# A fused macaron layer on one core: large tiles moved to multiples of 512 bytes, lone blocks rounded ahead of sums, rotary tables computed beside the down products

## The chip, the cores and the metric

One core of a Trainium2 chip runs the whole layer as one launch. The metric is device time in microseconds (us). The time before is 1897.17 us, the median of three runs (1897.16 to 1900.1).

## The reference, cut to what matters

Everything is float32; 256 tokens, model width 2048, feed-forward width 5632. The layer is a feed-forward block, a mixing block (retention with eight heads beside a sparse attention with eight heads), and a second feed-forward block, each with a residual sum.

```
def swiglu(h, w_gate, w_up, w_down):
    return (jax.nn.silu(h @ w_gate) * (h @ w_up)) @ w_down

x = x + 0.5 * swiglu(rmsnorm(x, ffn1_norm), w_gate1, w_up1, w_down1)
proj = rmsnorm(x, mix_norm) @ w_in                  # 2048 -> 6992 columns
rq, rk, rv, rg, aq, ak, av, iq, ik, iw = split(proj)
...
x = x + concatenate([ro, ao]) @ w_out
x = x + 0.5 * swiglu(rmsnorm(x, ffn2_norm), w_gate2, w_up2, w_down2)
return rmsnorm(x, final_norm)
```

`rq`, `rk`, `aq`, `ak`, `iq` and `ik` are rotated by position (`rope`), with cosines and sines of position times frequency, once for heads of 128 and once for heads of 64.

## The kernel before, in words

**Products.** Every float32 weight is read once from HBM by SP's queue, 1 MB at a time, into one of three `raw` buffers. A load is cut into pieces, and for each piece ScalarE (ACT) writes the rounded part `hi` (line 280) and VectorE (DVE) the rest `lo = raw - hi` (line 286), both in the one-pass format fp32r, into five buffers each. The activations are split in the same way. A product is then three TensorE (PE) matmuls, hi·hi, hi·lo and lo·hi, added up in PSUM: `run_mms` (line 232) with the weights streaming (512 columns each) and the activations stationary. In the input projections of the mixing block it is the other way round (`mm_cols`, lines 145 to 148: `hi` and `lo` stationary, `xg` streaming), save for two of them (`mm_rows`, lines 163 to 165).

**S and C pairs.** The products of the feed-forward blocks and of `w_out` take the depth in pairs of 256 rows. A C pair is done plainly, with 24 matmuls. An S pair follows Strassen's scheme with seven block products, 21 matmuls: DVE first forms four differences of weight blocks (line 272), and the activation side needs four sums besides the blocks that stand alone. `blocks_of` (lines 303 to 322) makes both sides of it for one pair: DVE forms the sums in `f`, ACT rounds the sums, ACT rounds the lone blocks, DVE subtracts twice. `left_pair` calls it for the products of a chunk after PE has transposed them (line 560).

**Order.** A feed-forward block has eleven chunks of 512 gate and 512 up columns, in two parts of six and five, and each part ends with its two down products. A chunk after the first has 3 S and 5 C pairs, 183 matmuls of 512 columns; the first is plain, 192. The product of a chunk is transposed and split in the middle of the next one (`sums_of`, `turning`); of its two pairs the first is an S pair in chunks one to four of each part, as the strings `DOWN` say. So 16 chunks in the two blocks have the split of an S pair in them, here called S-turn chunks. Everything is issued in an order fixed by hand: `after(step, ...)` hangs work on a piece, pieces are split four ahead of PE, and each engine runs its instructions in order.

**Addresses.** The built program places the tiles of a pool behind each other in the order of their first use. `gains` and `cst` stand ahead of `x0`, so that in pool `one` the large tiles (`x`, `xg`, `ext`, `ident`) begin 416 bytes past a multiple of 512; four small `r_tok` tiles at its end put `raw`, `hi`, `lo` and `mid` 32 bytes past one. Every operand of a large matmul is a whole number of 512-byte steps from its tile's start, so it has the same remainder (those of lines 163 to 165 with 272 columns excepted). `xg` and `ext` hold the activations for the gate, up and mixing products; `mid` holds those for the down products and `w_out`, and for three of the eight pairs of the first chunk.

**Tables.** `tables` (lines 641 to 681) computes angles, their reduction to one turn, and sines as a chain of DVE operations on 1024 elements, during the second part's first chunks of the first block; at that part's down product ACT's Sin writes them to `ext["rot"]`, in the space that the split `x` held until then.

Of the kernel before, what the change touches and what calls it, by code (L numbers as in the profile page):

```python
# [11 lines left out]
F32 = mybir.dt.float32  # L12
F32R = mybir.dt.float32r
I32 = mybir.dt.int32
AF = mybir.ActivationFunctionType
OP = mybir.AluOpType
# [3 lines left out]
P = 128  # L20
T = 256
# [20 lines left out]
C_TWO_PI = 2.0 * math.pi  # L42
C1 = 6.28125
C2 = round((C_TWO_PI - C1) * 2**17) / 2**17
C3 = C_TWO_PI - C1 - C2
MAGIC = 1.5 * 2**23
PI_DOWN = 3.1415925
# [3 lines left out]
def layer(ctx: ExitStack, tc: tile.TileContext, a: dict, out: bass.AP):  # L51
    nc = tc.nc
    V, S, G, TE = nc.vector, nc.scalar, nc.gpsimd, nc.tensor

    one = ctx.enter_context(tc.tile_pool(name="one", bufs=1))
    wts = ctx.enter_context(tc.tile_pool(name="wts", bufs=4))
    mid = ctx.enter_context(tc.tile_pool(name="mid", bufs=16))
    tmp = ctx.enter_context(tc.tile_pool(name="tmp", bufs=2))
    psum = ctx.enter_context(tc.tile_pool(name="psum", bufs=1, space=PSUM))
    ctx.enter_context(tc.manual_schedule())  # L60

# [2 lines left out]
    def new(pool, shape, dt=F32, tag=None, bufs=None):  # L64
        count[0] += 1
        kw = {} if bufs is None else {"bufs": bufs}
        return pool.tile(shape, dt, name=f"{tag}_{count[0]}", tag=tag, **kw)

    def half_k(tag, bufs=2):
        return new(tmp, [P, 2, T], F32, tag, bufs)  # L70

    def big(dt=F32, shape=(P, 4, T)):
        return new(mid, list(shape), dt, "mid")


    gains = new(one, [P, 3 * KT + NH], F32, "gains")
    cst = new(one, [P, 4 + NH], F32, "cst")
    x = [new(one, [P, D], F32, f"x{t}") for t in range(2)]
    xg = {}

# [6 lines left out]
    now, marks = [0], {}  # L87
# [16 lines left out]
    def after(step, fn):  # L104
        ends.setdefault(step, []).append(fn)
# [197 lines left out]
    def blocks_of(v, sums, alone):  # L303

        v = v.rearrange("p j (t n) -> p j t n", t=2)
        f = new(tmp, [P, 4, P], F32, "sq")
        V.tensor_tensor(f[:, 0], v[:, 0, 1], v[:, 1, 1], op=OP.add)
        V.tensor_tensor(f[:, 2], v[:, 0, 1], v[:, 0, 0], op=OP.subtract)
        V.tensor_tensor(f[:, 1], f[:, 0], v[:, 0, 0], op=OP.subtract)
        V.tensor_tensor(f[:, 3], v[:, 1, 0], f[:, 1], op=OP.subtract)  # L310
        vt = v.rearrange("p k t n -> p t k n")
        S.activation(sums[:, :, 0], f, AF.Copy)
        if alone.shape[1] == 4:
            a4 = alone.rearrange("p (t k) h n -> p t k h n", t=2)
            S.activation(a4[:, :, :, 0], vt, AF.Copy)  # L315
            V.tensor_tensor(a4[:, :, :, 1], vt, a4[:, :, :, 0].bitcast(F32), op=OP.subtract)  # L316
        else:
            for o, w in ((slice(0, 2), vt[:, 0]), (slice(2, 3), vt[:, 1, 1:2])):
                S.activation(alone[:, o, 0], w, AF.Copy)
                V.tensor_tensor(alone[:, o, 1], w, alone[:, o, 0].bitcast(F32), op=OP.subtract)  # L320
        V.tensor_tensor(sums[:, :, 1], f, sums[:, :, 0].bitcast(F32), op=OP.subtract)
        return sums, alone

    def left_pair(kind, v, in_psum=True):

        if kind == "S":
            if in_psum:
                f = half_k("b")
                S.activation(f, v, AF.Copy)
                v = f  # L330
            return blocks_of(v, big(F32R, (P, 4, 2, P)), big(F32R, (P, 4, 2, P)))
        t = big(F32R, (P, 2, 512))
        S.activation(t[:, :, :T], v, AF.Copy)
        V.tensor_tensor(t[:, :, T:], v, t[:, :, :T].bitcast(F32), op=OP.subtract)
        return t
# [18 lines left out]
    def s_of_x(c, norm, xT):  # L354
        v = half_k("b")
        for j in range(2):
            S.activation(v[:, j], xT[:, j], AF.Copy, scale=gain(norm, c, j))
        xs[c] = blocks_of(v, new(one, [P, 4, 2, P], F32R, f"xg{c}"), x_ext(c))
# [12 lines left out]
    ext = {}  # L371
# [7 lines left out]
    def mix_ext():  # L379
        t = new(one, [P, EXT], F32, "ext")  # L380
        at = 0
        for name, n in (("rot", 4 * T), ("avw", 2 * W_AV), ("ikT", T), ("score0", P), ("score1", T)):
            ext[name] = t[:, at:at + n]
            at += n
        ext["rot"] = ext["rot"].rearrange("p (k t) -> p k t", k=4)
        ext["avw"] = ext["avw"].rearrange("p (t n) -> p t n", t=2)
        ext["x"] = None
# [27 lines left out]
    def rsqrt(o, v, n):  # L415

        q = new(tmp, [P, 2 * NH], F32, "rs_q", 1)[:, :n]
        S.activation(q, v, AF.Sqrt)
        V.reciprocal(o, q)
        V.scalar_tensor_tensor(q, o, -0.5, o, op0=OP.mult, op1=OP.mult)  # L420
        V.tensor_tensor(q, q, v, op=OP.mult)
        V.scalar_tensor_tensor(o, q, 1.5, o, op0=OP.add, op1=OP.mult)

    def act_table(fn):

        t = new(tmp, [P, 1], F32, "table", 1)
        S.activation(t, ones[:, 0:1], fn)

    r_tok, r_of = {}, {}

    def row_of(tok):

# [9 lines left out]
    def rstd_tok(norm, ts=slice(0, 2)):  # L442
        v = new(tmp, [P, 2], F32, "sum_v", 1)[:, ts]
        s, k = squares[norm]
        V.tensor_reduce(v, s[:, ts, :k[ts.start]], axis=AX.X, op=OP.add)
        V.tensor_scalar(v, v, 1.0 / D, EPS, op0=OP.mult, op1=OP.add)
        if norm not in r_tok:
            r_tok[norm] = new(one, [P, 2], F32, f"r_tok{norm}")
        rsqrt(r_tok[norm][:, ts], v, ts.stop - ts.start)

    def rstd(norm):
        rstd_tok(norm)
        row = yield from row_of(r_tok[norm])
        r_of[norm] = new(tmp, [P, T], F32, "r", 1)
        S.activation(r_of[norm], row, AF.Copy)
# [182 lines left out]
    inv, sgn, kdec = cst[:, 0:2], cst[:, 2:4], cst[:, 4:4 + NH]  # L638


    def tables(at_sin):
        ang, n = big(), big()
        pi, pf = n[:, 0].bitcast(I32), n[:, 1]
        G.dma_start(pi, bass.AP(tensor=a["pos"].tensor, offset=a["pos"].offset, ap=[[0, P], [1, T]]))
        yield 3
        V.tensor_copy(pf, pi)
        for k in range(2):
            for j in range(2):
                V.tensor_scalar(ang[:, 2 * k + j], pf, inv[:, k:k + 1], None, op0=OP.mult)
        yield 3  # L650
        V.tensor_scalar(n, ang, 1.0 / C_TWO_PI, None, op0=OP.mult)
        yield 3
        for k in range(2):
            V.tensor_scalar(n[:, 2 * k], n[:, 2 * k], 0.25, None, op0=OP.add)
        yield 3
        V.tensor_scalar(n, n, MAGIC, None, op0=OP.add)
        yield 3
        V.tensor_scalar(n, n, MAGIC, None, op0=OP.subtract)
        for c in (C1, C2, C3):
            yield 3  # L660
            V.scalar_tensor_tensor(ang, n, -c, ang, op0=OP.mult, op1=OP.add)
        for k in range(2):
            V.tensor_scalar(ang[:, 2 * k], ang[:, 2 * k], math.pi / 2, None, op0=OP.add)
        yield 3

        V.tensor_scalar(n, ang, 1.0 / C_TWO_PI, MAGIC, op0=OP.mult, op1=OP.add)
        yield 3
        V.tensor_scalar(n, n, MAGIC, None, op0=OP.subtract)
        for c in (C1, C2, C3):
            yield 3  # L670
            V.scalar_tensor_tensor(ang, n, -c, ang, op0=OP.mult, op1=OP.add)
        yield 3
        V.tensor_scalar(ang, ang, PI_DOWN, -PI_DOWN, op0=OP.min, op1=OP.max)
        yield 3
        yield at_sin - now[0]
        mix_ext()
        rot = ext["rot"]
        S.activation(rot, ang, AF.Sin)
        yield 2
        for k in range(2):  # L680
            V.tensor_scalar(rot[:, 2 * k + 1], rot[:, 2 * k + 1], sgn[:, k:k + 1], None, op0=OP.mult)


    def first_squares():
        for t in range(2):
            nc.sync.dma_start(x[t], a["x"][t])
        yield 4
        for t in range(2):
            for c in range(2):
                square_x(0, t, 1024 * c, 1024)  # L690
                yield 1
        rstd_tok(0)

    after(FIRST_SQ, first_squares)
    end = ffn(1, 0, 1, False)
    after(marks[1, 1] + 2, lambda: tables(marks[1, 1, "down"] + 2))


    m0 = len(pieces)
# [355 lines left out]
    n = len(pieces)  # L1055
# [100 lines left out]
```

## Time and profile before

| | |
|---|---|
| median of three runs | 1897.17 us |
| the profiled execution: its time, its span | 1896.84 us, 1895.1 us |
| PE matmul, DVE, ACT busy | 98%, 87%, 57% of the span |
| DMA | 359 MB, 190 GB/s, engines busy half of the time |
| granted TensorE clock | 0.998 |

The page gives busy shares of the whole span. The timeline lists instructions of one engine with their start, so the distance from one matmul's start to the next is what a matmul takes in a row of them (its own duration overlaps the next). An idle time in brackets is the engine's wait before the instruction, with what ended it.

### The profile page before, as it was taken

Reading aid. Unit: us, or ns where it says so; the run is one execution under the profiler, and the core shown is the slowest. Engines: PE = TensorE matmul, PEld = TensorE weight load, DVE = VectorE, ACT = ScalarE, POOL = GpSimd, SP = SyncE. Lnnn points to the kernel's source line nnn. Section 1 sums busy time; section 2 is a strip of 40 time slices with the busy share of each in tenths; the row PEclk is TensorE's granted clock in tenths of the full one; section 3 lists DMA queues with packets and bytes.
Section 4 is the critical chain, followed back from the end, with each engine's and each line's share of the span. In section 5 each row is a group of like instructions: output and inputs, shape, how many; then the busy total and the mean of one; then the engine's idle time right before and its main releaser. Section 6 shows DMA issues by size and latency. Waiting matters only on the chain.

```text
span 1895.1 us, 22782 instructions
## 1 busy us (share of the span) xinstructions
PE 1862.9 (98%) x8643; PEld 1525.0 (80%) x8643; DVE 1646.2 (87%) x2109; ACT 1072.9 (57%) x1351; POOL 5.3 (0%) x14
## 2 busy tenths in 40 slices
PE   9999999999999999999999999999999999999997
PEld 7877788887777787988888888877778888777786
DVE  7899998889999997789865786799999889999998
ACT  7655555545555565656654566555555455555564
POOL 0000000000000000000000000000000000000000
PEclk9999999999999999999999999999999999999999
DMA  8544556545455454545434364545554555445554
GB/s 312 199 178 178 199 197 221 194 173 195 182 201 197 165 212 156 188 164 207 178 137 174 134 222 156 200 178 196 201 200 180 200 200 200 178 181 202 194 180 176
DMA packets 51885, 359.33 MB, mean 190 GB/s; under 512 B 5920, under 2 KB 5920, under 8 KB 9280
## 3 DMA queue, kind: packets, MB, share of 16 engines
q1 hardware_dynamic: 50976, 355.62, 50.7%
q8 instruction: 67, 1.10, 0.2%
q10 hardware_dynamic: 432, 1.08, 0.2%
q0 software_dynamic: 368, 1.19, 0.2%
q14 instruction: 42, 0.34, 0.0%
HBM read 355.76 MB, written 2.10 MB: 189 GB/s over the span
## 4 chain that ended last, share of the span: by engine, by line
PE 75%; DVE 19%; ACT 3%; issue 2%; DMA 0%; SPq 0%; DVEq 0%; ACTq 0%
PE M L232 58%; DVE lo L286 8%; PE M L146 8%; PE M L148 4%; DVE raw L272 3%; DVE e L471 2%; ACT hi L280 1%; DVE s L471 1%; PE M L164 1%; PE M L165 1%; PE M L163 1%; DVE x L468 1%; PE M L560 1%; DVE mid L316 1%; ACT mid L315 1%
## 5 line engine op out<-in xcount | busy, mean ns | idle before, releaser
L280 ACT ACTIVATE hi<-raw 128x1024 fp32r<-128x1024 f32 (+2 forms) x859 | 848.3, 1008 | 567.0 <-DVE raw L272 366.4
L286 DVE TENSOR_TENSOR lo<-raw,hi 128x1024 fp32r<-128x1024 f32 (+2 forms) x859 | 978.3, 1159 | 121.9 <-ACT hi L280 107.9
L232 PE MATMUL M<-hi,xg 128*128 128x512 f32 x2240 | 739.2, 396 | 1.4 <-DVE e L471 1.0
L232 PE MATMUL M<-hi,mid 128*128 128x512 f32 x1690 | 528.2, 391 | 4.1 <-DVE e L986 1.7
L232 PEld LDWEIGHTS M<-hi,xg 128*128 128x128 f32 x2240 | 421.7, 188 | 102.8 <-DVE e L471 5.3
L232 PE MATMUL M<-lo,xg 128*128 128x512 f32 x1120 | 443.6, 396 | 5.8 <-DVE lo L286 5.7
L232 PEld LDWEIGHTS M<-hi,mid 128*128 128x128 f32 x1690 | 317.2, 188 | 73.8 <-DVE e L986 2.1
L232 PE MATMUL M<-lo,mid 128*128 128x512 f32 x845 | 329.5, 390 | 1.5 <-DVE lo L286 1.4
L272 DVE TENSOR_TENSOR raw<-raw 128x512 f32<-128x512 f32 x380 | 262.9, 692 | 12.7
L232 PEld LDWEIGHTS M<-lo,xg 128*128 128x128 f32 x1120 | 211.0, 188 | 60.3 <-DVE lo L286 13.0
L146 PE MATMUL M<-xg,hi 128*128 128x512 f32 x688 | 245.1, 398 | 1.2 <-DVE xg L300 1.1
L232 PEld LDWEIGHTS M<-lo,mid 128*128 128x128 f32 x845 | 158.7, 188 | 35.9 <-DVE lo L286 3.5
L148 PE MATMUL M<-xg,lo 128*128 128x256 f32 x645 | 182.1, 282 | 0.0
L146 PEld LDWEIGHTS M<-xg,hi 128*128 128x128 f32 x688 | 128.3, 188 | 30.4 <-DVE xg L300 1.8
L232 PE MATMUL M<-hi,ext 128*128 128x512 f32 x360 | 143.5, 399 | 1.9
L148 PEld LDWEIGHTS M<-xg,lo 128*128 128x128 f32 x645 | 121.3, 188 | 0.8
L232 PEld LDWEIGHTS M<-hi,ext 128*128 128x128 f32 x360 | 67.8, 188 | 23.2 <-DVE s L471 8.0
L232 PE MATMUL M<-lo,ext 128*128 128x512 f32 x180 | 71.1, 395 | 0.0
L471 DVE TENSOR_TENSOR s<-s,M 128x512 f32<-128x512 f32 x98 | 65.5, 683 | 2.2 <-PE M L232 1.2
L550 ACT ACTIVATE s<-s,r_tok 128x512 f32<-128x512 f32 x40 | 27.1, 720 | 54.6 <-DVE s L471 54.6
L471 DVE TENSOR_TENSOR e<-s,M 128x512 f32<-128x512 f32 x58 | 39.6, 684 | 1.0
L232 PEld LDWEIGHTS M<-lo,ext 128*128 128x128 f32 x180 | 33.9, 188 | 7.4
(175 smaller groups left out, 923.7 us busy)
## 6 DMA issues: line engine op xcount, KB each, us to landing
raw<-in_wgu SPq DMA_DIRECT2D x175, 1024.0 KB, 4.8
raw<-in_wd SPq DMA_DIRECT2D x88, 1024.0 KB, 4.8
raw<-in_w_out SPq DMA_DIRECT2D x16, 1024.0 KB, 4.8
raw<-in_w_iq SPq DMA_DIRECT2D x8, 1024.0 KB, 4.8
raw<-in_w_aq SPq DMA_DIRECT2D x8, 1024.0 KB, 4.8
raw<-in_w_rk SPq DMA_DIRECT2D x8, 1024.0 KB, 4.9
raw<-in_w_rq SPq DMA_DIRECT2D x8, 1024.0 KB, 4.8
raw<-in_w_rv SPq DMA_DIRECT2D x8, 1024.0 KB, 4.8
```

The lines of the kernel that those rows point to most:

```text
L146: TE.matmul(acc, lhsT=hi[:, c:c + P], rhs=r, start=st, stop=sp)
L148: TE.matmul(acc[:, T:], lhsT=lo[:, c:c + P], rhs=r[:, :T], start=False, stop=False)
L163: TE.matmul(o, lhsT=h, rhs=hi[:, i * n:(i + 1) * n], start=st, stop=False)
L164: TE.matmul(o, lhsT=h, rhs=lo[:, i * n:(i + 1) * n], start=False, stop=False)
L165: TE.matmul(o, lhsT=l, rhs=hi[:, i * n:(i + 1) * n], start=False, stop=sp)
L232: TE.matmul(bank[m], lhsT=p["left"](pair, a)[u], rhs=split_of[i][v][:, off:off + 512], start=st, stop=sp)
L272: V.tensor_tensor(r[:, o:o + 512], r[:, a:a + 512], r[:, b:b + 512], op=OP.subtract)
L280: S.activation(hi[:, :p["n"]], raw, AF.Copy)
L286: V.tensor_tensor(lo[:, :p["n"]], raw, hi[:, :p["n"]].bitcast(F32), op=OP.subtract)
L315: S.activation(a4[:, :, :, 0], vt, AF.Copy)
L471: V.tensor_tensor(o, a, b, op=OP.add)
L550: S.activation(u[b], bank[SUM[b]] if plain else u[b], AF.Silu, scale=r_tok[norm][:, t:t + 1])
```

## The change

It has three parts. (1) The four `r_tok` tiles are placed ahead of `x`, and a tile `pad` of 480 bytes that nobody uses behind them. In the built program `x`, `xg`, `ext`, `ident`, `raw`, `hi`, `lo` and `mid` then all begin at multiples of 512 bytes; the small scratch tiles `b`, `e`, `sq` move from 64 to 32 bytes past one, `s` from 192 to 160. (2) `blocks_of` rounds the lone blocks on ACT before DVE forms the sums, and DVE's subtraction for the lone blocks comes before that for the sums. (3) `tables` works in two halves of 512 elements in the scratch tiles `b` and `sq`, beginning in the first part's down product, writes each half to DRAM by ACT's queue, and `load_tables` reads both back into `ext["rot"]` in the second part's down product.

```diff
     gains = new(one, [P, 3 * KT + NH], F32, "gains")
     cst = new(one, [P, 4 + NH], F32, "cst")
+    r_tok = {n: new(one, [P, 2], F32, f"r_tok{n}") for n in range(4)}
+    new(one, [P, 120], F32, "pad")
     x = [new(one, [P, D], F32, f"x{t}") for t in range(2)]
...
     def blocks_of(v, sums, alone):
         v = v.rearrange("p j (t n) -> p j t n", t=2)
+        vt = v.rearrange("p k t n -> p t k n")
+        if alone.shape[1] == 4:
+            a4 = alone.rearrange("p (t k) h n -> p t k h n", t=2)
+            parts = [(vt, a4[:, :, :, 0], a4[:, :, :, 1])]
...
+        for w, hi, lo in parts:
+            S.activation(hi, w, AF.Copy)
         f = new(tmp, [P, 4, P], F32, "sq")
         V.tensor_tensor(f[:, 0], v[:, 0, 1], v[:, 1, 1], op=OP.add)
...
         S.activation(sums[:, :, 0], f, AF.Copy)
-        if alone.shape[1] == 4:
-            a4 = alone.rearrange("p (t k) h n -> p t k h n", t=2)
-            S.activation(a4[:, :, :, 0], vt, AF.Copy)
-            V.tensor_tensor(a4[:, :, :, 1], vt, a4[:, :, :, 0].bitcast(F32), op=OP.subtract)
...
+        for w, hi, lo in parts:
+            V.tensor_tensor(lo, w, hi.bitcast(F32), op=OP.subtract)
         V.tensor_tensor(sums[:, :, 1], f, sums[:, :, 0].bitcast(F32), op=OP.subtract)
...
-    def tables(at_sin):
-        ang, n = big(), big()
...
+    rot_dram = new(dram, [P, 4, T], F32, "rot_dram")
+    def tables():
         for k in range(2):
+            ang, n = half_k("b"), half_k("sq")
+            pi, pf = n[:, 0].bitcast(I32), n[:, 1]
+            G.dma_start(pi, bass.AP(tensor=a["pos"].tensor, offset=a["pos"].offset, ap=[[0, P], [1, T]]))
+            yield 3
...
+            S.activation(ang, ang, AF.Sin)
+            yield 1
+            V.tensor_scalar(ang[:, 1], ang[:, 1], sgn[:, k:k + 1], None, op0=OP.mult)
+            nc.scalar.dma_start(rot_dram[:, 2 * k:2 * k + 2], ang)
+        act_table(AF.Silu)
+    def load_tables():
         mix_ext()
-        rot = ext["rot"]
-        S.activation(rot, ang, AF.Sin)
...
+        nc.scalar.dma_start(ext["rot"], rot_dram)
...
-    after(marks[1, 1] + 2, lambda: tables(marks[1, 1, "down"] + 2))
+    after(marks[1, 0, "down"] + 6, tables)
+    after(marks[1, 1, "down"] + 4, load_tables)
```

The instructions of PE and of SP keep their kinds and order; ACT and DVE change at these places.

ACT, the split of an S pair in an S-turn chunk, before (`b` is the transposed product, `sq` holds the sums, line 312 rounds the sums, line 315 the lone blocks, line 333 belongs to the C pair behind):

```order
165 L329 ACTIVATE b_1800<-M_5_76 128x512
166 L312 ACTIVATE mid_1802<-sq_1804 128x4x128
167 L315 ACTIVATE mid_1803<-b_1800 128x4x128
168 L333 ACTIVATE mid_1817<-M_7_78 128x2x256
169 L280 ACTIVATE hi_1820<-raw_1733 128x1024
```

and now:

```order
165 L333 ACTIVATE b_1807<-M_10_83 128x512
166 L316 ACTIVATE mid_1810<-b_1807 128x4x128
167 L322 ACTIVATE mid_1809<-sq_1812 128x4x128
168 L337 ACTIVATE mid_1824<-M_12_85 128x2x256
169 L283 ACTIVATE hi_1827<-raw_1740 128x1024
```

The rounding of the lone blocks, which needs only `b`, has moved ahead of that of the sums, which waits for DVE.

DVE, third S pair of the first part's first down product, now (before, only the rows of lines 272 and 286, which are 275 and 289 here, stood there; `sq` and `b` are the tables' scratch):

```order
292 L289 TENSOR_TENSOR lo_2361<-raw_2278,hi_2360 128x1024
293 L651 CAST sq_2334<-sq_2334 128x256
294 L653 TENSOR_SCALAR b_2333<-sq_2334,cst_75 128x256 x2
295 L275 TENSOR_TENSOR raw_2278<-raw_2278 128x512 x3
296 L289 TENSOR_TENSOR lo_2375<-raw_2278,hi_2374 128x1024
297 L655 TENSOR_SCALAR sq_2334<-b_2333 128x512
298 L656 TENSOR_SCALAR sq_2334<-sq_2334 128x256
299 L275 TENSOR_TENSOR raw_2278<-raw_2278 128x512
300 L289 TENSOR_TENSOR lo_2386<-raw_2278,hi_2385 128x1024
301 L658 TENSOR_SCALAR sq_2334<-sq_2334 128x512
302 L659 TENSOR_SCALAR sq_2334<-sq_2334 128x512
303 L289 TENSOR_TENSOR lo_2405<-raw_2278,hi_2404 128x512
```

One or two table operations now stand between the splits of each piece. The first half ends in the second C pair behind this one, and the second half lies over the C pairs at the end of this product and the first S pair of the next.

## Rows read from the trace of the kernel before

**Rows 1.** The page's first part: busy time, share, instructions.
```profile
PE 1862.9 (98%) x8643; PEld 1525.0 (80%) x8643; DVE 1646.2 (87%) x2109; ACT 1072.9 (57%) x1351; POOL 5.3 (0%) x14
```

**Rows 2.** Timeline of PE, first chunk: start us, us, line, operands, count.
```profile
17.06 0.39 PE L232 MATMUL M<-lo,mid 128*128 128x512 f32 x1
...
20.69 0.40 PE L232 MATMUL M<-hi,mid 128*128 128x512 f32 x1
20.92 0.40 PE L232 MATMUL M<-hi,xg 128*128 128x512 f32 x1
...
26.28 0.40 PE L232 MATMUL M<-hi,xg 128*128 128x512 f32 x1
```

**Rows 3.** Timeline of PE, an S-turn chunk's front: first and last of 98 starts.
```profile
193.34 0.39 PE L232 MATMUL M<-hi,xg 128*128 128x512 f32 x1
...
215.88 0.39 PE L232 MATMUL M<-lo,xg 128*128 128x512 f32 x1
```

**Rows 4.** Windows: an S-turn chunk with tables, one without; us, busy (instructions) by engine.
```profile
455.00:499.30 44.30, 38.91 (x168) 30.25 (x166) 42.54 (x56) 22.74 (x28) 0.00 (x0) 1.00 0.45 168
499.30:543.80 44.50, 44.08 (x191) 35.05 (x191) 41.58 (x52) 24.77 (x30) 0.00 (x0) 1.00 0.50 189
```

**Rows 5.** Timeline of DVE, S-turn chunk.
```profile
175.36 0.69 DVE L316 TENSOR_TENSOR mid<-b,mid 128x512 fp32r<-128x512 f32 x1 [1.22 <-ACT mid L315]
...
177.17 1.22 DVE L286 TENSOR_TENSOR lo<-raw,hi 128x1024 fp32r<-128x1024 f32 x1
```

**Rows 6.** Timeline of ACT, the same place.
```profile
172.49 0.60 ACT L329 ACTIVATE b<-M 128x512 f32<-128x512 f32 x1 [1.03 <-PE M L560]
174.18 0.63 ACT L312 ACTIVATE mid<-sq 128x512 fp32r<-128x512 f32 x1 [1.09 <-DVE sq L310]
...
175.71 2.00 ACT L280 ACTIVATE hi<-raw 128x1024 fp32r<-128x1024 f32 x2
```

**Rows 7.** Timeline of PE, end of that chunk's stretch behind the transposes.
```profile
188.67 0.40 PE L232 MATMUL M<-hi,xg 128*128 128x512 f32 x1
189.19 0.50 PE L232 MATMUL M<-hi,ext 128*128 128x512 f32 x1
...
192.77 0.50 PE L232 MATMUL M<-lo,xg 128*128 128x512 f32 x1 [0.31 <-DVE lo L286]
```

**Rows 8.** The chain that ended last, 140 to 196 us.
```profile
148.28 23.74 PE M L232 x101
```

**Rows 9.** Timeline of PE, input projections: first and last of 29 pairs.
```profile
932.03 0.40 PE L146 MATMUL M<-xg,hi 128*128 128x512 f32 x1
...
942.22 0.27 PE L145 MATMUL M<-xg,lo 128*128 128x256 f32 x1
```

**Rows 10.** The page's groups of line 232, PE alone: count, busy us, mean ns.
```profile
L232 PE MATMUL M<-hi,xg 128*128 128x512 f32 x2240 | 739.2, 396 | 1.4 <-DVE e L471 1.0
L232 PE MATMUL M<-hi,mid 128*128 128x512 f32 x1690 | 528.2, 391 | 4.1 <-DVE e L986 1.7
...
L232 PE MATMUL M<-lo,xg 128*128 128x512 f32 x1120 | 443.6, 396 | 5.8 <-DVE lo L286 5.7
...
L232 PE MATMUL M<-lo,mid 128*128 128x512 f32 x845 | 329.5, 390 | 1.5 <-DVE lo L286 1.4
...
L232 PE MATMUL M<-hi,ext 128*128 128x512 f32 x360 | 143.5, 399 | 1.9
...
L232 PE MATMUL M<-lo,ext 128*128 128x512 f32 x180 | 71.1, 395 | 0.0
```

**Rows 11.** Groups by shape between 757 and 1075 us, PE.
```profile
L163 PE MATMUL M<-hi,xg 128*128 128x512 f32 x64 | 25.7, 402 | 0.0
```

**Rows 12.** Groups of DVE between 440 and 700 us: the tables.
```profile
L661 DVE SCALAR_TENSOR_TENSOR mid<-mid,mid 128x1024 f32<-128x1024 f32 x3 | 3.7, 1219 | 0.0
```

**Rows 13.** Timeline of DVE, first part's down product: a C pair's split.
```profile
297.43 2.59 DVE L286 TENSOR_TENSOR lo<-raw,hi 128x1024 fp32r<-128x1024 f32 x2 [0.48 <-ACT hi L280]
```

**Rows 14.** Timeline of PE: first use of the first `lo` of rows 13.
```profile
301.07 0.39 PE L232 MATMUL M<-lo,mid 128*128 128x512 f32 x1
```

More of the change, by code (lines that the diff above doesn't have):

```diff
@@ L58, in layer @@
     tmp = ctx.enter_context(tc.tile_pool(name="tmp", bufs=2))
+    dram = ctx.enter_context(tc.tile_pool(name="dram", bufs=1, space=bass.MemoryType.DRAM))
     psum = ctx.enter_context(tc.tile_pool(name="psum", bufs=1, space=PSUM))
@@ L305, in blocks_of @@
         v = v.rearrange("p j (t n) -> p j t n", t=2)
+        vt = v.rearrange("p k t n -> p t k n")
+        if alone.shape[1] == 4:
+            a4 = alone.rearrange("p (t k) h n -> p t k h n", t=2)
+            parts = [(vt, a4[:, :, :, 0], a4[:, :, :, 1])]
+        else:
+            parts = [(vt[:, 0], alone[:, :2, 0], alone[:, :2, 1]), (vt[:, 1, 1:2], alone[:, 2:, 0], alone[:, 2:, 1])]
+        for w, hi, lo in parts:
+            S.activation(hi, w, AF.Copy)
         f = new(tmp, [P, 4, P], F32, "sq")
@@ L310, in blocks_of @@
         V.tensor_tensor(f[:, 3], v[:, 1, 0], f[:, 1], op=OP.subtract)
-        vt = v.rearrange("p k t n -> p t k n")
         S.activation(sums[:, :, 0], f, AF.Copy)
-        if alone.shape[1] == 4:
-            a4 = alone.rearrange("p (t k) h n -> p t k h n", t=2)
-            S.activation(a4[:, :, :, 0], vt, AF.Copy)
-            V.tensor_tensor(a4[:, :, :, 1], vt, a4[:, :, :, 0].bitcast(F32), op=OP.subtract)
[L317 to L320, printed above, removed]
+        for w, hi, lo in parts:
+            V.tensor_tensor(lo, w, hi.bitcast(F32), op=OP.subtract)
         V.tensor_tensor(sums[:, :, 1], f, sums[:, :, 0].bitcast(F32), op=OP.subtract)
@@ L427, in act_table @@
         S.activation(t, ones[:, 0:1], fn)
-    r_tok, r_of = {}, {}
+    r_of = {}
     def row_of(tok):
@@ L446, in rstd_tok @@
         V.tensor_scalar(v, v, 1.0 / D, EPS, op0=OP.mult, op1=OP.add)
-        if norm not in r_tok:
-            r_tok[norm] = new(one, [P, 2], F32, f"r_tok{norm}")
         rsqrt(r_tok[norm][:, ts], v, ts.stop - ts.start)
@@ L638, in layer @@
     inv, sgn, kdec = cst[:, 0:2], cst[:, 2:4], cst[:, 4:4 + NH]
-    def tables(at_sin):
-        ang, n = big(), big()
[L643 to L646, printed above, removed]
-        for k in range(2):
-            for j in range(2):
[L649 to L675, printed above, removed]
-        mix_ext()
-        rot = ext["rot"]
-        S.activation(rot, ang, AF.Sin)
-        yield 2
-        for k in range(2):
-            V.tensor_scalar(rot[:, 2 * k + 1], rot[:, 2 * k + 1], sgn[:, k:k + 1], None, op0=OP.mult)
@@ new lines, in layer @@
+    rot_dram = new(dram, [P, 4, T], F32, "rot_dram")
+    def tables():
+        for k in range(2):
+            ang, n = half_k("b"), half_k("sq")
+            pi, pf = n[:, 0].bitcast(I32), n[:, 1]
+            G.dma_start(pi, bass.AP(tensor=a["pos"].tensor, offset=a["pos"].offset, ap=[[0, P], [1, T]]))
+            yield 3
+            V.tensor_copy(pf, pi)
+            for j in range(2):
+                V.tensor_scalar(ang[:, j], pf, inv[:, k:k + 1], None, op0=OP.mult)
+            yield 1
+            V.tensor_scalar(n, ang, 1.0 / C_TWO_PI, None, op0=OP.mult)
+            V.tensor_scalar(n[:, 0], n[:, 0], 0.25, None, op0=OP.add)
+            yield 1
+            V.tensor_scalar(n, n, MAGIC, None, op0=OP.add)
+            V.tensor_scalar(n, n, MAGIC, None, op0=OP.subtract)
+            for c in (C1, C2, C3):
+                yield 1
+                V.scalar_tensor_tensor(ang, n, -c, ang, op0=OP.mult, op1=OP.add)
+            V.tensor_scalar(ang[:, 0], ang[:, 0], math.pi / 2, None, op0=OP.add)
+            yield 1
+            V.tensor_scalar(n, ang, 1.0 / C_TWO_PI, MAGIC, op0=OP.mult, op1=OP.add)
+            V.tensor_scalar(n, n, MAGIC, None, op0=OP.subtract)
+            for c in (C1, C2, C3):
+                yield 1
+                V.scalar_tensor_tensor(ang, n, -c, ang, op0=OP.mult, op1=OP.add)
+            yield 1
+            V.tensor_scalar(ang, ang, PI_DOWN, -PI_DOWN, op0=OP.min, op1=OP.max)
+            S.activation(ang, ang, AF.Sin)
+            yield 1
+            V.tensor_scalar(ang[:, 1], ang[:, 1], sgn[:, k:k + 1], None, op0=OP.mult)
+            nc.scalar.dma_start(rot_dram[:, 2 * k:2 * k + 2], ang)
+        act_table(AF.Silu)
```

## The prediction, made before the change was run

> **What bounds it now.** I read the busy shares first. PE is busy for 98% of the span, DVE for 87% and ACT for 57% [rows 1], so the time is what the matmuls take one behind the other, and little else. Two questions are left: what one matmul takes, and where PE waits at all.
>
> The first is answered by starts in a row of matmuls without a wait. In the first chunk, 16 matmuls whose stationary operand lies in `mid` start between 17.06 and 20.69 us, 226.9 ns each; the next 23, with the stationary operand in `xg`, start between 20.92 and 26.28 us, 233.0 ns each [rows 2]. Line, shape, streaming tiles and chunk are the same. What differs is the tile, and with it the remainder of its address: 32 bytes past a multiple of 512 for `mid`, 416 for `xg`, with the streaming `hi` and `lo` at 32 in both. In the front of a later chunk, `xg` and `ext` again, 97 steps from 193.34 to 215.88 us take 232.4 each [rows 3]; I count 232.5 from here on. The granted clock is at its upper level, 2.4 GHz, throughout, so the clock isn't the cause.
>
> The second: an S-turn chunk takes 44.5 us, in which DVE is busy for 41.6 [rows 4]. At its turn DVE stands idle for 1.22 us on the lone blocks [rows 5], while ACT itself waits 1.09 us for the sums [rows 6]; from there DVE is the late one, and PE pays at the end of the stretch, with 0.30 us ahead of 189.19 (520 ns between starts where 230 would do), 0.31 of idle time ahead of 192.77 (0.46 against the usual distance), and three gaps of 0.1 around them [rows 7], 1.05 us in all. The front of such a chunk, 23.7 us behind 148.28, is PE alone [rows 8].
>
> **Part 1, addresses.** Bounds first. The trace has no large matmul with both operands at remainder 0. It has remainders 32 and 32 (226.7 to 227), streaming 32 and stationary 416 (232 to 233), and, in the input projections, streaming 416 and stationary 32: 29 pairs of 512 and 256 columns between 932.03 and 942.22 us, 351 ns a pair [rows 9]. I take it that what counts is where the two operands stand to each other, modulo 512. Then 0 and 0 is like 32 and 32: `mid` stays at 227, and `xg` and `ext` come down to it, by 5.5 ns. There are 2240 + 1120 + 360 + 180 = 3900 of them [rows 10], 21.5 us if PE is the bound at all of them; how much of that is kept is counted with part 2. The pairs of the input projections would take 226.7 for the long one and as much over the columns for the short one as now, some 347: 4 to 5 ns on 688 pairs (21 chunks of 32 and one of 16, by the code), 3 us. The three times 64 long matmuls of lines 163 to 165 [rows 11] have `xg` stationary: 192 by 5.5 ns, 1 us.
>
> The row says that the stationary tile's place costs a running matmul 6 ns. The Trainium skill (TensorE: Matmul & The Clock Gate, Step-by-step: what each phase is for) says the opposite, that TensorE reads both operands by independent ports and that loading the next weights takes nothing from the running matmul. By that rule part 1 is worth nothing; it is the second rival below, and the rows of the first chunk speak against it.
>
> What else lies at other addresses? The small scratch tiles go from 64 to 32 past a multiple. DVE takes 0.69 us for 512 elements that read such a tile [rows 5], and I expect no change: the operations on `raw`, at 32 now, are no slower. I put it at nothing, between -1 and +1 us.
>
> **Part 2, lone blocks.** Now ACT rounds the lone blocks from 173.10, when `b` is there, to 173.7, and the sums from 174.2; DVE takes the lone blocks at 174.2, straight behind its sums, in place of 175.36. That would be 1.2 us, but the next split waits for ACT: its three roundings behind 174.2 (0.63, 0.58 and 1.05 us) end at 176.4, where the split of 177.17 starts at 177.26 in the chain. So 0.84 us earlier. Of PE's 1.05 us this saves about 0.6, because the last 2.6 us (rounding and split behind a buffer that PE releases) stay a fixed chain: 16 times 0.6, 9.6 us, if matmuls stay as they are.
>
> With matmuls 5.5 ns shorter PE comes to that point earlier and the whole 0.84 counts, while the 82 matmuls between the transposes and 192.77 give nothing more, since DVE is late there. The 101 matmuls in front [rows 8] give 0.55. That is 1.4 us per S-turn chunk, 16 times: 22.4 us for parts 1 and 2 together. The four later chunks without that turn have no such wait: 183 matmuls by 5.5 ns is 1.0, of which I keep 0.8, 3.2 us. The two plain chunks have five of eight pairs in `xg`: 120 by 5.5 less what DVE eats, 1.2 us for both.
>
> **Part 3, tables.** Removed: the window with the tables holds 168 matmuls in 44.3 us, the next 191 in 44.5 [rows 4]; less one for the shorter window, 22 missing ones at 233 ns are 5.1 us. Added: 15 to 16 us of DVE work in the down products, since an operation on 1024 elements (1.22 us [rows 12]) becomes two on 512, at 0.6 to 0.7 us (0.69 for a subtraction of that length [rows 5]), and short ones come on top. In a period of an S and a C pair there DVE idles for only 0.48 us, and a split is ready 2.4 us before PE wants it (297.43 + 1.22, and 301.07) [rows 13, 14]. The first half puts 7 us into little over two periods: lag over 2.4 us falls to PE. Going through it piece by piece I get 3 us of waiting, in the fourth S pair and the C pair behind; the second half finds C pairs with over 5 us in hand and costs nothing. Bounds: 0, and 7. Sin and Silu load no table between them in either order of instructions. The three transfers through DRAM take ACT's queue; behind the first two waits a rounding, until DVE has done the table's last row, inside the 3 us. The read back stands where PE has long left `ext`. Net: -2.1 us.
>
> **Sum.** 22.4 + 3.2 + 1.2 + 1.0 + 3.0 + 2.1 = 32.9 us less than the profiled execution's 1896.84, which stands 0.3 us under the median of the runs: **1864 us**.
>
> **Rivals.**
> 1. *Both tiles gain.* The 32 bytes cost something too, and `mid` comes down by as much as `xg`, to 221, and `xg` with it. For: if the place of a tile costs 6 ns, some of the 227 may be of that kind too. Against: matmuls at 32 and 32 are even to 1 ns, with no sign of collisions. S-turn chunks gain only in the front part (16 times 0.55, 9 us), other chunks 6, 2361 matmuls of the down products and `w_out` by 5.7 ns 13, the projections 6: 34 us more, **1830**. The Trainium skill (same page, Wait — 56ns, not 53.3ns?) gives 215.7 ns for 512 columns back to back; by it, as an estimate, the sum would be some 1800, with DVE the bound in most chunks.
> 2. *Addresses do nothing.* `xg` is slow for another reason, such as how its matmuls are mixed. Then parts 2 and 3 are left: 9.6 + 2.1, **1885**. Against: the rows of the first chunk.
> 3. *Slower: remainder 0 is a bad place.* If it is the address itself and not the distance that counts, both operands at 0 can be as bad as 416, or worse. `xg` stays, `mid` rises to 232.5: 2535 matmuls [rows 10] by 5.5 are 14 us, against 11.7 saved: **1899**. It decides from the point where `mid` takes over 231.5 ns. Both at 238 would be 2535 by 11 and 3900 by 5.5, 49 us, 1935; I hold that for remote.
>
> **Chances.** The forecast 0.58, rival 1 0.15, rival 2 0.12, rival 3 0.15. The forecast's own range is 1855 to 1874 (tables 0 to 7, part 2 between 0.6 and 1.2 each). For 8 in 10 I take in rival 2 and half of each of the others: 1830 to 1892. A measurement of this kernel can tell about 0.2%, 3.8 us, from no change: faster by more 0.82 (forecast, rival 1 and most of rival 2), within it 0.05 (the rest of rival 2 and the mild end of rival 3), slower 0.13.
>
> **What would show it.** Part 1: starts on `xg` 227 ns apart in the first chunk, beside 227 on `mid`, and pairs of 347 in the projections. Part 2: DVE's 1.22 us of idle time ahead of the lone blocks gone, S-turn chunks of 43.1 us. Part 3: the chunk at 455 us as long as its neighbours, and waits of PE on `lo` of some 3 us between 290 and 330 us. It is wrong if `xg` still stands at 232, if `mid` moves by more than 2 ns, or if the down product with the tables grows by over 7 us.

## The result, and the profile after

The changed kernel takes 1872.48 us (median of 4 runs, 1870.88 to 1873.38), beside 1897.63 us for the kernel before on the same chip: a ratio of 0.9864, with a 95% interval from 0.9847 to 0.9881. That is 25.2 us less; the forecast was 33 less, 1864, with a range from 1830 to 1892.

The span is 1871.6 us. In the page's first part PE has lost 24 us, and the others stand where they stood [rows 1]:

```profile
PE 1838.7 (98%) x8643; PEld 1524.3 (81%) x8643; DVE 1647.2 (88%) x2122; ACT 1074.0 (57%) x1353; POOL 5.8 (0%) x15
```

PE's timeline of the first chunk answers to [rows 2]. The line of the matmuls is 235 now (it was 232).

```profile
18.32 0.62 PE L235 MATMUL M<-hi,mid 128*128 128x512 f32 x2
...
21.05 0.39 PE L235 MATMUL M<-hi,mid 128*128 128x512 f32 x1
21.27 0.39 PE L235 MATMUL M<-hi,xg 128*128 128x512 f32 x1
...
26.49 0.39 PE L235 MATMUL M<-hi,xg 128*128 128x512 f32 x1
```

Between the two `xg` rows lie 23 steps of 227.0 ns (233.0 before); between those of `mid`, 12 steps of 227.5, as before. So `xg` came down to `mid`, and `mid` stayed.

The chain that ended last, through one S-turn chunk (its columns are start, us, what):

```profile
145.04 23.19 PE M L235 x101
...
185.88 1.05 ACT hi L283
...
186.96 1.24 DVE lo L289
...
188.24 1.88 PE M L235 x7
```

From 145.04 to 188.24 is 43.2 us (44.5 before, 43.1 forecast). The 101 matmuls in front take 23.19 us where they took 23.74 [rows 8]. Behind the turn the chain still goes through a rounding and a split.

DVE and ACT at the turn, which answer to [rows 5, 6]. DVE:

```profile
170.41 0.68 DVE L324 TENSOR_TENSOR mid<-b,mid 128x512 fp32r<-128x512 f32 x1
171.19 0.69 DVE L325 TENSOR_TENSOR mid<-sq,mid 128x512 fp32r<-128x512 f32 x1
```

ACT:

```profile
169.34 0.63 ACT L316 ACTIVATE mid<-b 128x512 fp32r<-128x512 f32 x1
170.53 0.63 ACT L322 ACTIVATE mid<-sq 128x512 fp32r<-128x512 f32 x1 [0.56 <-DVE sq L321]
```

DVE's 1.22 us of idle time ahead of the lone blocks is gone, and ACT's wait for the sums has halved from 1.09 to 0.56 us, with the lone blocks' rounding in the other half.

So far the forecast. The tables did not follow it. In the first part's down product the profile now has a hole. ACT:

```profile
307.51 0.63 ACT L673 ACTIVATE b<-b 128x512 f32<-128x512 f32 x1 [2.75 <-DVE b L672]
...
310.70 0.33 ACTq L676 DMA_DIRECT2D rot_dram<-b  x1
311.13 2.00 ACT L283 ACTIVATE hi<-raw 128x1024 fp32r<-128x1024 f32 x2 [2.04 <-DVE b L675]
313.04 0.58 ACT L478 ACTIVATE s<-M 128x512 f32<-128x512 f32 x1
```

DVE, same place:

```profile
309.12 1.22 DVE L289 TENSOR_TENSOR lo<-raw,hi 128x1024 fp32r<-128x1024 f32 x1 [1.65 <-ACT hi L283]
310.27 0.35 DVE L675 TENSOR_SCALAR b<-b,cst 128x256 f32<-128x256 f32 x1
312.22 2.36 DVE L289 TENSOR_TENSOR lo<-raw,hi 128x1024 fp32r<-128x1024 f32 x2 [1.61 <-ACT hi L283]
```

PE, same place:

```profile
309.63 0.40 PE L235 MATMUL M<-hi,mid 128*128 128x512 f32 x1
313.67 1.12 PE L562 MATMUL M<-ident,e 128*128 128x128 f32 x4 [3.65 <-ACT s L478]
...
316.00 0.78 PE L235 MATMUL M<-hi,mid 128*128 128x512 f32 x1
...
319.04 0.40 PE L235 MATMUL M<-lo,mid 128*128 128x512 f32 x1
```

The circle reads like this. ACT's Sin (line 673) stands 2.75 us for DVE's last clamp. The rounding behind it comes late, so DVE stands 1.65 us for `hi`, and its last table row (line 675) is late too. ACT's DMA issue waits 2.04 us for that row. The roundings and the copy of `M1` (line 478) that stand behind the issue are late, and PE's transposes need that copy: 3.65 us. Behind this wait the granted clock, in windows of 6 us, is 0.76 and then 0.67, and from 316.00 to 319.04 seven matmuls start 434 ns apart on the mean, where 227 is usual: the lower level of 1.2 GHz, 1.45 us more.

### The profile page after: what moved, and what is told of

It is laid out like the page before. It is cut to its first block, busy times and chain, and to the rows that moved or that the text cites. A ratio compares the mean times of both kernels' runs of the same rounds, so it can differ in the third digit from the quotient of the medians.

```text
span 1871.6 us, 22796 instructions
## 1 busy us (share of the span) xinstructions
PE 1838.7 (98%) x8643; PEld 1524.3 (81%) x8643; DVE 1647.2 (88%) x2122; ACT 1074.0 (57%) x1353; POOL 5.8 (0%) x15
## 4 chain that ended last, share of the span: by engine, by line
PE 83%; DVE 11%; ACT 3%; issue 1%; DMA 1%; ACTq 0%; SPq 0%; DVEq 0%
PE M L235 66%; PE M L149 8%; DVE lo L289 6%; PE M L151 4%; ACT hi L283 2%; DVE raw L275 2%; PE M L562 1%; PE M L168 1%; PE M L167 1%; PE M L166 1%; DVE x L470 1%; DMA e<-in_xT 0%; PE M L820 0%; ACT sq L412 0%; DVE e L473 0%
## 5 line engine op out<-in xcount | busy, mean ns | idle before, releaser
L235 PE MATMUL M<-hi,xg 128*128 128x512 f32 x2240 | 726.0, 390 | 0.2 <-ACT hi L283 0.2
L235 PE MATMUL M<-lo,xg 128*128 128x512 f32 x1120 | 437.9, 391 | 5.6 <-DVE lo L289 5.6
L235 PEld LDWEIGHTS M<-lo,xg 128*128 128x128 f32 x1120 | 210.3, 188 | 55.0 <-DVE lo L289 12.2
L734 ACT ACTIVATE b<-e 64x512 f32<-64x512 f32 (+2 forms) x46 | 28.2, 612 | 20.2 <-DVE e L720 19.7
```

Source lines behind the costliest of these rows:

```text
L235: TE.matmul(bank[m], lhsT=p["left"](pair, a)[u], rhs=split_of[i][v][:, off:off + 512], start=st, stop=sp)
L734: S.activation(b[p0:p0 + w], q[p1:p1 + w], AF.Copy)
```

## The experiments

**The parts apart.** Four kernels each take a part of the change, with the edits of the diff above: part 1 alone, part 2 alone, parts 1 and 2 (tables as before), part 3 alone.

Part 1 alone. 

> The kernel before with the address part alone. Theory 1 (the distance of the two operands counts, modulo 512): matmuls on xg and ext start 227 ns apart in place of 232.5, mid stays at 227; but behind the turn of an S-turn chunk DVE is late without the reordering, so that only the 101 matmuls in front gain, 0.55 us in each of 16 such chunks, and some 5 us come from the plain chunks, the later ones and lines 163 to 165: about 1883 us (-14). If it comes to 1875 or less, the wait at the turn shrinks by itself and the two parts are not tied to each other as the prediction had it. Rival 2 (addresses do nothing): 1897, the whole gain being the reordering's.

Part 2 alone. 

> The kernel before with the reordering of the lone blocks alone. Theory 1: 0.6 us in each of 16 S-turn chunks, 1888 us (-9.6), an S-turn chunk of 43.9 us, xg still at 232.5 ns. Rival (PE is the bound there, and the waits only move): under 3 us gained, 1895 or more.

Parts 1 and 2. 

> The changed kernel with the tables as before: addresses and reordering. Theory 1: the tables of the changed kernel cost some 11.5 us in the first part's down product and save 5.5 in the chunk where they stood, so that this kernel is faster than the changed one, about 1866 us. The prediction's terms 22.4 + 3.2 + 1.2 + 1.0, without the 3.0 of the projections, give 1870. Rival (the half clock and the waits in the down product come from the faster matmuls and not from the tables): this kernel has them too, and it takes 1878.

Part 3 alone. 

> The kernel before with the new tables alone. Theory 1 (the moved tables cost more than they save, because ACT stands behind the tables' Sin and DMA): slower than before, 1902 to 1904 us, with PE's wait of some 4 us at the transposes and a stretch at half clock in the first part's down product. The prediction's term, -5.1 + 3: 1895. Rival (they only hurt when matmuls are faster): 1892 to 1896, no half clock.

| kernel | us | ratio to before, 95% interval | difference | S-turn period |
|---|---|---|---|---|
| part 1, addresses | 1885.68 | 0.9933, 0.9920 to 0.9945 | -12.4 | 44.0 us |
| part 2, lone blocks | 1882.08 | 0.9916, 0.9902 to 0.9929 | -16.0 | 43.6 us |
| parts 1 and 2 | 1869.27 | 0.9852, 0.9837 to 0.9867 | -28.8 | 43.1 us |
| part 3, tables | 1904.05 | 1.0030, 1.0018 to 1.0041 | +5.9 | 44.5 us |

(The kernel before had 1898.11 us on that chip.) Parts 1 and 2 add up almost to the microsecond, 28.5 against 28.8. Part 1 alone came out 2 us short of its expectation; part 2 alone gave 16 us where 9.6 were expected. Part 3 by itself makes the kernel slower, as theory 1 of its expectation has it. It does so with the slow matmuls of before, so the waits in the down product aren't due to faster ones: the list of PE's waits in that stretch (what waits, what for, us in all, times, longest) is the same in both kernels.

Changed kernel, 254 to 476 us:

```profile
PE M L562 <- ACT s L478: 3.6, 1, 3.6
PE M L235 <- DVE lo L289: 3.0, 5, 0.9
PE M L562 <- DVE s L473: 0.4, 1, 0.4
```

Part 3 alone, 262 to 486 us:

```profile
PE M L561 <- ACT s L477: 3.7, 1, 3.7
PE M L233 <- DVE lo L287: 3.0, 5, 0.9
...
```

Parts 1 and 2, tables where they were, 254 to 470 us:

```profile
PE M L561 <- DVE s L472: 2.8, 1, 2.8
PE M L234 <- DVE lo L288: 2.0, 2, 1.7
```

7.0 us of waits and 1.45 of half clock have taken the place of 4.8 us. That is 3.7 us lost, and the runs say 3.2 (1872.48 less 1869.27).

**Is it the distance, or the multiple of 512?** Both kernels here have parts 1 and 2, with the tables as before. The first leaves out the filler, so that all large tiles begin at 32 past a multiple:

```diff
-    new(one, [P, 120], F32, "pad")
```

> Addresses and reordering, tables as before, but without the 480 bytes of filler: the four small tiles alone stand ahead of x, and x, xg, ext, raw, hi, lo and mid all begin 32 bytes past a multiple of 512. Theory 1 (only the distance of the two operands counts): as with the filler, 1869 us within 2, xg and mid both 227 ns apart. Rival (multiples of 512 themselves count): xg at 232, and 1882, what the reordering alone gives.

The second, too, has no filler, and puts 64 bytes ahead of each `xg` tile but the first:

```diff
-    new(one, [P, 120], F32, "pad")
-    xg = {}
+    xg, gaps = {}, {}
+
+    def gap(c):
+        if c and c not in gaps:
+            gaps[c] = new(one, [P, 16], F32, f"gap{c}")
...
+            gap(c)
             t = new(one, [P, 2, 512], F32R, f"xg{c}")
```

> As the kernel without filler, with 64 bytes put ahead of each of xg1 to xg7, so that the stationary tiles xg0 to xg7 begin 0, 64, 128, 192, 256, 320, 384 and 448 bytes (modulo 512) past hi, lo and mid, and ext 64. Theory 1: xg0 and mid 227 ns; xg6, the distance of the kernel before, 232.5; of the others nothing is known, and if the cost is one of being apart at all, they are at 232 too, which leaves some 1880 us in all. If the cost is of one special distance, only xg6 and its neighbours are slow, 1871. Rival (the tile or its part of memory counts, not the distance): xg0 to xg7 all alike.

Without the filler: 1869.65 us, ratio 0.9852 (0.9838 to 0.9865), the same as with it. No tile has to begin at a multiple of 512; moving the four small tiles was enough, which shifts `x`, `xg` and `ext` by 128 bytes, from 416 past a multiple to 32. The kernel with gaps takes 1879.14 us, ratio 0.9901 (0.9886 to 0.9916). Its first chunk goes through the tiles one behind the other, 24 matmuls each, in the order `xg2`, `mid`, `xg4`, `mid`, `xg6`, `xg7`:

```profile
21.19 0.40 PE L237 MATMUL M<-hi,xg 128*128 128x512 f32 x1
...
26.78 0.39 PE L237 MATMUL M<-hi,mid 128*128 128x512 f32 x1
...
32.23 0.39 PE L237 MATMUL M<-hi,xg 128*128 128x512 f32 x1
...
37.67 0.39 PE L237 MATMUL M<-hi,mid 128*128 128x512 f32 x1
...
43.12 0.40 PE L237 MATMUL M<-hi,xg 128*128 128x512 f32 x1
...
48.47 0.62 PE L237 MATMUL M<-hi,xg 128*128 128x512 f32 x2
...
54.20 0.39 PE L237 MATMUL M<-hi,ext 128*128 128x512 f32 x1
```

`xg2`, 128 bytes off: 232.9 ns a step. `mid`: 227.1. `xg4`, 256 off: 226.7. `mid` again: 227.1. `xg6`, 384 off: 232.6 (23 steps to 48.47). `xg7`, 448 off: 229.2 (25 steps, the first still `xg6`). Over the whole run, the mean distance from one start to the next within a tile (those under 245 ns, 219 or more of each):

```
distance   0    64   128   192   256   320   384   448
mean ns  228.0 233.2 232.3 230.0 229.0 233.4 232.8 228.9
```

At 0 and 256 the median is 227. Streaming tiles, shape and line are the same in all of them, and the tiles `xg2` and `xg6`, slow here, ran at 227 without the gaps, so it is the place that costs, not the tile and not the multiple. Theory 1 fits, with one thing that it had not said: 256 bytes off has the same median as 0. One rival is left. No kernel moved the streaming tiles alone in these matmuls, so a cost of the stationary tile's own remainder, nothing at 0 and at 32, would fit the rows as well. Only the input projections speak against it: there the stationary `hi` and `lo` stand at 32 before and without the filler, `xg` streams, and the pairs went from 351 ns [rows 9] to 347 in some stretches and 353 in others.

**ACT's queue, or DVE's time?** The change's tables, with the Sin alone two pieces later, and with both the Sin and the write to DRAM two pieces later. The work is the same:

```diff
             V.tensor_scalar(ang, ang, PI_DOWN, -PI_DOWN, op0=OP.min, op1=OP.max)
+            yield 2
             S.activation(ang, ang, AF.Sin)
             yield 1
             V.tensor_scalar(ang[:, 1], ang[:, 1], sgn[:, k:k + 1], None, op0=OP.mult)
+            yield 2
             nc.scalar.dma_start(rot_dram[:, 2 * k:2 * k + 2], ang)
```

The Sin alone (the first `yield 2`). 

> The changed kernel with the Sin alone two pieces later; the write to DRAM still stands right behind DVE's last row. It parts the two waits in ACT's queue, 2.75 us of the Sin and 2.04 us of the transfer, whose sum theory 1 holds for the wait of 3.8 us at the transposes and the half clock behind it. If each counts by itself: about 1869, half way between the changed kernel (1872.5) and the one with both moved (1866.6). If the Sin's is the one that matters: 1866 to 1867.5. If the transfer's: 1871.5 or more.

Both. 

> The changed kernel, with the Sin two pieces later behind DVE's clamping, and the write to DRAM two pieces later behind DVE's last row. The same work on each engine. Theory 1 (ACT, waiting in its queue for DVE's table rows, holds up the roundings and the copy that PE's transposes wait for): the wait of 3.65 us at the transposes and the stretch at half clock go, some 5 us less than the changed kernel, 1867.5. Rival (DVE has no room for 15 us of table work there, whoever waits): 1871 to 1874, as the changed kernel.

The Sin alone: 1868.98 us, ratio 0.9842 (0.9829 to 0.9856), half way as the first reading had it. Both: 1866.57 us, ratio 0.9834 (0.9820 to 0.9847), 5.9 us less than the changed kernel. In the second one ACT's Sin waits 0.85 us, the DMA issue not at all, and the copy of `M1` stands at 308.72 where it stood at 313.04:

```profile
307.23 0.63 ACT L674 ACTIVATE b<-b 128x512 f32<-128x512 f32 x1 [0.85 <-DVE b L672]
...
308.72 0.58 ACT L478 ACTIVATE s<-M 128x512 f32<-128x512 f32 x1
```

PE's waits there, 254 to 470 us, are all on DVE now:

```profile
PE M L235 <- DVE lo L289: 2.0, 4, 0.7
PE M L562 <- DVE s L473: 1.4, 1, 1.4
```

So the table steps' place in ACT's order cost 6 us, and the rest is DVE's.

**DVE's place.** The same kernel, with the two halves begun where two runs of C pairs are near:

```diff
+            if k:
+                yield marks[1, 0, "down"] + 46 - now[0]
             ang, n = half_k("b"), half_k("sq")
...
-    after(marks[1, 0, "down"] + 6, tables)
+    after(marks[1, 0, "down"] + 16, tables)
```

> The kernel with the later Sin and the later writes, and with the two halves of the tables begun at the 16th and the 46th piece of the down products in place of the 6th and right behind each other, so that DVE's table rows lie between the splits of the two runs of C pairs, not between those of S pairs. Theory 1 (what is left of the tables' cost, 5 us of PE's waits on lo and at the transposes, comes from DVE, which has no idle time among S pairs and over 4 us of it in each run of C pairs): 1862 to 1863.5, 3 to 4.5 us less than with the later Sin alone. Rival (DVE's 15 us cost the same wherever they stand, since DVE is busy for 90% of these products): 1866 or more.

1862.77 us, ratio 0.9810 (0.9796 to 0.9823): 36 us under the kernel before, some 10 under the changed one, and 3.8 under the one with both steps moved (1866.57). It is also 6.5 us under parts 1 and 2 with the tables as before (1869.27), so the tables' move pays, and by more than the 2.1 us of the forecast, once its steps stand where the engines have room. The windows show where DVE found room. Parts 1 and 2 with the tables as before, the first run of C pairs, where DVE is busy for 14.85 of 18 us (the third of the busy times):

```profile
312.00:330.00 18.00, 18.00 (x81) 14.88 (x81) 14.85 (x18) 7.00 (x7) 0.00 (x0) 1.00 0.45 168
```

This kernel, the same run, with 17.76 of 18 us:

```profile
312.00:330.00 18.00, 18.00 (x81) 14.92 (x80) 17.76 (x27) 7.50 (x8) 0.00 (x0) 1.00 0.50 175
```

PE is busy without a break in both. Of its waits between 254 and 470 us one is left:

```profile
PE M L562 <- DVE s L473: 1.5, 1, 1.5
```

**Tables on POOL, a miss.** The changed kernel, with the tables' arithmetic on POOL:

```diff
-            V.tensor_copy(pf, pi)
+            G.tensor_copy(pf, pi)
...
+            yield 14
             S.activation(ang, ang, AF.Sin)
...
-            nc.scalar.dma_start(rot_dram[:, 2 * k:2 * k + 2], ang)
+            G.dma_start(rot_dram[:, 2 * k:2 * k + 2], ang)
```

> The changed kernel, with the tables' arithmetic on POOL, which is idle, in pieces of 256 elements, the two writes to DRAM on POOL's queue and the Sin 14 pieces behind. Theory 1 (the tables' cost in the down product is the time they take from DVE and, through waits in queues, from ACT): PE's waits of some 8.6 us there go, and the chunk where the tables stood before stays short; 1864 to 1865. Rival (POOL works at the cost of DVE, through their common access to memory): DVE's splits take longer than 1.22 us for 1024 elements beside POOL's work, and the time is 1868 or more.

1884.35 us, ratio 0.9926 (0.9914 to 0.9939), 12 us more than the changed kernel. Most of that is the edit's own fault: POOL is slower than was allowed for, and ACT's second Sin, put 14 pieces behind, stood for it,

```profile
364.07 0.63 ACT L675 ACTIVATE b<-b 128x512 f32<-128x512 f32 x1 [15.24 <-POOL b L673]
```

and the rounding behind it came late: PE's longest wait for it is 12.2 us, DVE's 14.3. But the rival showed as well. POOL had run the first half ahead, as soon as its buffers were free, beside two S-turn chunks, which took 45.8 and 47.0 us in place of 43.2. DVE's groups there, 170 to 212 us, first of this kernel:

```profile
L289 DVE TENSOR_TENSOR lo<-raw,hi 128x1024 fp32r<-128x1024 f32 x16 | 21.1, 1345 | 0.1
L275 DVE TENSOR_TENSOR raw<-raw 128x512 f32<-128x512 f32 x12 | 10.3, 856 | 0.4
L473 DVE TENSOR_TENSOR s<-s,M 128x512 f32<-128x512 f32 x3 | 2.0, 682 | 0.0
```

and of the changed kernel:

```profile
L289 DVE TENSOR_TENSOR lo<-raw,hi 128x1024 fp32r<-128x1024 f32 x19 | 22.8, 1221 | 0.9 <-ACT hi L283 0.5
L275 DVE TENSOR_TENSOR raw<-raw 128x512 f32<-128x512 f32 x12 | 8.3, 692 | 0.4
L473 DVE TENSOR_TENSOR s<-s,M 128x512 f32<-128x512 f32 x4 | 2.6, 681 | 0.0
```

Subtractions of two tiles in SBUF take 10 and 24% longer beside POOL (three short splits of 512 elements 36%, 930 ns for 684); the one that reads PSUM for its second operand takes the same. The Trainium skill (SBUF — State Buffer, SBUF: two separate sides) has such a rule: POOL and a DVE instruction with two SBUF inputs share one pair of ports, which one of them holds for its whole instruction. The trace agrees on which operations are hit. How fast the kernel would be with a later Sin on POOL wasn't tried.

## Why the prediction was right, and where it was wrong

From the transposes of the first S-turn chunk to those of the fifth are 172.7 us, where it was 178.0: four periods, 1.33 us less in each, 21.3 in 16. The table sets the terms of the sum against the runs:

| term, us saved | predicted | measured | from |
|---|---|---|---|
| parts 1 and 2, 16 S-turn chunks | 22.4 | 21.3 | the period |
| projections | 3.0 | 0.6 | 0.9 ns less a pair on the mean, 688 pairs |
| other chunks, plain chunks, long matmuls | 5.4 | 6.9 | what is left of 28.8, not measured apart |
| tables | 2.1 | -3.2 | with and without part 3 |
| sum | 32.9 | 25.6 | the runs: 25.2 |

**Part 1** was right in its size and in where it acts: `mid` unmoved, `xg` 5.5 to 6 ns shorter, 0.55 us in the front of an S-turn chunk. Its assumption that the operands' distance counts fits every kernel here, with the rival named above still open. The second rival, "addresses do nothing", is out: part 1 alone gave 12.4 us. The rule of the Trainium skill that stood beside it (TensorE: Matmul & The Clock Gate, Step-by-step: what each phase is for; independent ports for both operands) does not cover these rows: where the stationary tile lies changes what the running matmuls take. The third rival, remainder 0 itself, is out by the kernel without filler. The first, a gain in `mid`, is out by `mid` at 227.

The step on the **projections** failed. It took pairs of 347 ns from the long matmul's 226.7 and a shorter one in proportion. Some stretches do run so, others at 353; the last section has the rows. On the mean next to nothing is gained.

**Part 2** was right in sum, wrong in how it divides. "Of PE's 1.05 us this saves about 0.6, because the last 2.6 us ... stay a fixed chain": alone it saved 0.9 us a chunk. The distances between starts, over the usual one, add up to 1.2 us of waiting in an S-turn chunk before, and to 0.3 with part 2 alone. The 0.46 us over the usual distance ahead of 192.77 [rows 7] are 0.11 there; PE, part 2 alone, the same two matmuls:

```profile
189.42 0.39 PE L232 MATMUL M<-hi,xg 128*128 128x512 f32 x1
189.76 0.50 PE L232 MATMUL M<-lo,xg 128*128 128x512 f32 x1
```

So that chain wasn't fixed: DVE's lateness ran through to it, and went. With part 1 added PE comes sooner and half a microsecond of it is back, which is why the sum of 1.4 a chunk still fits (1.33).

**Part 3** is where the sum failed, by 5.3 of the 8.5 us by which the forecast was too low (0.8 of the 8.5 is the kernel before, 1897.63 where the forecast began from 1896.84). The term was "3 us of waiting" added, bounds 0 and 7, with the transfers' wait "inside the 3 us". Measured are 7.0 us of waits and 1.45 of half clock, over the upper bound. The prediction followed DVE's lag alone, and there it was not far off: with ACT freed, 3.4 us of waits are left. What it missed is that ACT is a queue. It noted that a rounding stands behind the transfer, but not that the Sin stands there as well, each waiting for DVE; that DVE in turn waits for the roundings behind them; and that the copy for PE's transposes is in the same queue. The second half, which was to cost nothing in C pairs "with over 5 us in hand", ends in the same circle (ACT waits 2.36 us for the clamp and 1.99 us for the last row), and PE pays 1.1 us of the list behind it. One of the prediction's own signs of being wrong was met here: from the fifth set of transposes to the seventh, the stretch of the two down products, PE takes 221.3 us in place of 213.2, and the limit was 7 more. Of the waits on `lo` that it expected between 290 and 330 us, some 3, there are 1.9; the larger wait is the one on ACT. That C pairs have the room was right: with the halves put there, both together leave 1.5 us.

The removal was worth about what was forecast (5.1 us; 4.8 of listed waits with the faster matmuls).

Two figures of the prediction don't come out when worked again, and neither changes the forecast. With its own parts, tables at 7 us and part 2 at 0.6, the upper end of the forecast's own range is 1872, not 1874, so the measured 1872.5 stands at its edge. In the first rival the matmuls of the down products and `w_out` are 2391, not 2361, which is 0.2 us.

## What to carry to other kernels

Where matmuls of the same shape take two different times, compare the addresses of their operands: here a distance of 384 bytes, modulo 512, cost 2.4% of a matmul, and four small tiles moved ahead took it away. An instruction that waits for another engine costs what stands behind it in its queue, so a side job's waiting step goes in only when what it waits for is done by then; two pieces of delay were worth 6 us here. And work to be hidden goes where the engine that does it has idle time, read from windows of the stage, not where there is room for its buffers.

## What the runs showed of the hardware

In the kernel with gaps, beside the 227 ns of `mid`, a stationary tile 64, 128, 320 or 384 bytes (modulo 512) from the streaming one costs 5 to 6.5 ns of a matmul of 512 columns, and 192 and 448 cost 2 to 3. At 256 the median is the 227 of 0 and the mean 1 ns above that of `xg` at 0. Whether it is the distance or the stationary tile's own remainder that counts, and why, no run here shows for certain.

In the input projections, where `xg` streams and `hi` and `lo` are stationary, all at distance 0, the pairs of 512 and 256 columns run at one of two paces. Changed kernel, PE, first and last short matmul of 29 pairs, twice:

```profile
758.11 0.28 PE L151 MATMUL M<-xg,lo 128*128 128x256 f32 x1
...
768.16 0.28 PE L151 MATMUL M<-xg,lo 128*128 128x256 f32 x1
...
769.20 0.28 PE L151 MATMUL M<-xg,lo 128*128 128x256 f32 x1
...
779.45 0.28 PE L151 MATMUL M<-xg,lo 128*128 128x256 f32 x1
```

That is 346.6 ns a pair in the first stretch and 353.4 in the second, held all through; before, all stretches had 350 to 351 [rows 9]. The same stretch of the program has one pace in one kernel and the other in another: the first of these two runs at 347 here and at 353 in the kernel with parts 1 and 2 alone. What picks the pace stays open.
